# A two-layer decoder trunk: the order and the engines of norms, softmax weights and low parts

## The chip, the cores and the metric

The kernel runs on one core of a Trainium2 chip. A core has a matrix engine (TensorE, PE in the profile, with its weight loads as PEld), a vector engine (VectorE, DVE), an engine for activation functions (ScalarE, ACT), a general engine (GpSimd, POOL) and an engine that mostly issues transfers (SyncE, SP). They work side by side and wait for one another by semaphores. They share an on-chip memory (SBUF) of 128 partitions; matmuls write into eight accumulation banks (PSUM), each 128 partitions by 512 float32 values. The metric is the device time of one execution in microseconds (us), the median of several runs; lower is better.

## The reference, cut to what matters

```python
def ffn(h, w_in, w_out):            # four of these, each added with weight 0.5
    g, u = split(h @ w_in, 2)       # 1024 -> 2 x 2816
    return (silu(g) * u) @ w_out

for i in range(2):                  # 512 tokens, 1024 features, float32
    h = h + 0.5 * ffn(rmsnorm(h, nw[0]), ...)
    hn = rmsnorm(h, nw[1])
    h = h + (retention(hn) if i == 0 else forgetting_attention(hn))
    h = h + 0.5 * ffn(rmsnorm(h, nw[2]), ...)
    gate = sigmoid(rmsnorm(h, nw[3]) @ ple_w_gate[i])
    h = h + gate * (p[i] @ ple_w_proj[i])      # 256 -> 1024
return rmsnorm(h, final_norm_w)
```

Retention has four heads, with queries and keys of 256 and values of 512 features. Queries and keys are rotated by position, each head's output is normalised by its own root mean square over its 512 features (`rmsnorm(o, gn_w)`), multiplied by `silu(g)` and projected back. Forgetting attention has sixteen heads of 64 features: softmax over `q k^T * 64^-0.5 + c[query] - c[key]`, where `c` is a running sum of the logarithms of forget gates, causal, times `v`, and projected back.

## The kernel before, in words

Activations lie transposed, eight blocks of 128 features by 512 tokens (`h`, `hall`). Every matmul operand is split into a high part, rounded to the fast matmul type (float32r), and a low part that holds the rest; a product is three matmuls, high times high, high times low and low times high (`mm3`, L298 to L300). `split` (L289, L290) makes the parts of an activation: ScalarE copies the high part, VectorE subtracts. A third form with a scale is L292, L293.

The order of the whole is feed-forward 0, retention, feed-forward 1, gated input 0, feed-forward 2, forgetting attention, feed-forward 3, gated input 1 (in two halves of the tokens), final norm. TensorE executes in the order in which the program is written. The instructions of the other engines, whose queues are also worked off in order, are ordered by a planner that goes by its own estimate of when their inputs are ready.

**Weights** come through a class that holds the plan, a list of all weight chunks in the order of use (`W.plan`). A chunk of 128 x 1024 is loaded by a transfer that SyncE issues into one of four raw buffers (`wraw`), ScalarE casts its high part (L78), and VectorE or GpSimd, whichever `W.low` names at that point, subtracts for the low part (L79). There are three buffers of split chunks (`w8`), so the preparation runs two chunks ahead (`LOOKAHEAD`).

**Feed-forward input products** use a Strassen-Winograd form: `product` (L480) multiplies by a weight pair (`Pair`: the quarters q and r of a 1024 x 256 slab, with VectorE sums of them, `emit_sums`, L140, L78 and L79 on `sums`), in the steps `start`, `one`, `two`, `three`, `finish`. L530 to L533 and L546 to L548 are the sums on results, in place in the bank. Before them come a few pairs in the plain form (`plain`, L511; two in layers 0, 2 and 3, none in layer 1). There are 22 pairs of each layer, used up in chunks, and after each chunk the output products (`out_blocks`, L572, L575). A pair's low part is made in one of two ways: a *direct* pair by L79, like a chunk; any other by a ScalarE copy of the high part (L116), a ScalarE negation into the low half (L117) and an accumulating transfer that GpSimd issues, which adds the raw weights from HBM (L118). Direct are the first Winograd pair of a layer and one pair at each border of chunks.

**Norms** (`Norm`): squares are summed over the feature blocks by VectorE and GpSimd (`acc`, L414), split, and summed over the partitions by eight small matmuls with a vector of ones, 128 tokens each (`columns`, L428), so that the result has tokens on partitions, four columns (128 x 4). L459 and L452 to L456 form the inverse root there: two steps of Newton's kind behind ScalarE's root and VectorE's reciprocal (L453). `rows` then spreads the columns over partitions by four matmuls with a diagonal (`spread`, L447) into a bank, which ScalarE copies (L441) to a 128 x 512 tile `n.r`.

**Retention** goes head by head: q and k products and their rotation (`rotate`, L703 to L705), values (`v_part`, L683 to L685), the gates (`gate`, L781, L783), scores, chunk outputs `os` in four banks, the sum of their squares (`squares`, L715, L719), `head_scale`, then `outputs` (L810, L814 and a split). In `head_scale` two matmuls with a full matrix of ones over 512 columns (`over_features`, L310, L311) leave the sum in every partition, and the whole inverse root runs on 128 x 512 tiles; EPS, scaled by the token's mean square, is kept as a tile `epsv`. `early` is the number of gates ahead of `os`. Heads 2 and 3 are projected back together (`OutBoth`: `first` with head 2's half of the features, `rest` with head 3's and the additions to `h`, L669). `outputs` of a head come after the next head's first products.

**Attention** runs in eight passes `p` of two heads each. A pass multiplies out keys (`k_part`: L909 scales the result by `n.r` into a temporary tile in SBUF, L913 and L914 cast the high part, L915 subtracts) and queries (`q_part`: L925, L931, L932 likewise), then the scores (L948 with the low parts of the keys, L951), with four query blocks of 128, 256, 384 or 512 keys for each head. In `softmax` VectorE subtracts the row of `c` and takes the maximum on the way (L970, L974, custom instructions), flips the maximum's sign (L979), ScalarE takes the exponential with a running sum (L980), VectorE takes the reciprocal (L981) and scales the weights (L982). TensorE turns the weights (L997), L289 and L290 split them, and `attend` multiplies them by the values (L1010, L1011; L1013, L1014 combine the parts). Between these steps stand those of the next pass, with the preparation of its weights.

**The gated input** (`ple`): a gate block is a product of the normed `h` with `ple_gate` (24 matmuls), its own block a product of `p` with `ple_proj` (two feature blocks, six matmuls), and `rest` scales the gate by `n.r`, takes the sigmoid (L1089) and adds the product to `h` (L1093). In the first part gates 0 and 1 come ahead of `columns` and gate 2 ahead of `rows`, and each own product stands in its `rest`. `final_scale` and the final norm (L1129, L1146 to L1154) follow in layer 1.

## Time and profile before

| what | value |
|---|---|
| runs, us | 2286.51, 2284.73, 2275.85 |
| median of the runs, us | 2284.73 |
| profiled execution, its own time, us | 2285.92 |
| its span, first to last instruction, us | 2284.1 |
| mean granted clock of TensorE | 0.978 |
| busy, share of the span | PE 95%, DVE 67%, ACT 52%, POOL 20% |
| bytes read from HBM | 266.91 MB, 118 GB/s over the span |

The profile comes from one execution recorded by the hardware. A row of the timeline gives the start and the length in us, the engine, the line of the kernel, the operation, output and inputs with their shapes, how many instructions the row joins, and in square brackets how long the engine had been idle before and what it waited for. A row of the groups gives total busy time and the mean of one in ns, then the idle time before them. A row of the windows gives a stretch, its length, the busy us of PE, PEld, DVE, ACT and POOL with their instructions, the granted clock of TensorE (1.00 is full speed), the busy share of the transfer engines and GB/s. Matmuls overlap, so that the length of one is more than the distance between two.

### The profile page before, as it was taken

The page shows a single profiled execution, that of the slowest core. Times are in us where ns is not written, and L with a number is a line of the kernel's source. Part 1 is how long each engine was busy: PE and PEld are TensorE (multiplying, and loading weights), DVE is VectorE, ACT ScalarE, POOL GpSimd, SP SyncE. Part 2 cuts the span into 40 slices and gives each one's busy share as a digit, 9 for nine tenths or more (in the row PEclk, how much of TensorE's full clock was granted, in tenths as well). Part 3 has the DMA queues.
Part 4 walks back from the last instruction along what each step waited for, and adds up shares of the span by engine and source line. Part 5 has one row for each costly group of instructions (what it writes and reads, how often), then busy time and mean ns, then how long its engine had stood idle before and what let it go on. Part 6 is the DMA issues. An engine that isn't in the chain of part 4 may idle for free.

```text
span 2284.1 us, 34483 instructions
## 1 busy us (share of the span) xinstructions
PE 2170.2 (95%) x13465; PEld 1950.0 (85%) x13465; DVE 1530.0 (67%) x2775; ACT 1195.3 (52%) x1993; POOL 453.6 (20%) x339
## 2 busy tenths in 40 slices
PE   7999999999999899999998999999899989999998
PEld 7898997888888798989877898988777789989978
DVE  8676766374463976767675676765886776867674
ACT  7464553433333673646465464644665564645553
POOL 0010013444343010101100010113323100101044
PEclk8999999999999999999998999999899999999999
DMA  6465563222222474646333464653222144655531
GB/s 185 106 168 146 144 158 93 81 95 83 93 83 75 120 164 130 159 125 159 113 97 100 126 161 133 157 128 98 85 74 79 61 120 116 167 139 144 147 102 38
DMA packets 86610, 271.26 MB, mean 119 GB/s; under 512 B 9504, under 2 KB 13088, under 8 KB 86448
## 3 DMA queue, kind: packets, MB, share of 16 engines
q1 hardware_dynamic: 63328, 209.78, 28.0%
q0 software_dynamic: 21888, 58.21, 15.1%
q8 instruction: 105, 1.72, 0.3%
q10 hardware_dynamic: 1232, 1.09, 0.1%
q14 instruction: 57, 0.47, 0.1%
HBM read 266.91 MB, written 2.13 MB: 118 GB/s over the span
## 4 chain that ended last, share of the span: by engine, by line
PE 76%; DVE 11%; ACT 5%; DMA 4%; issue 3%; POOL 1%; SPq 0%; ACTq 0%; DVEq 0%; POOLq 0%
PE bank L480 29%; PE bank L300 13%; PE bank L298 13%; PE bank L299 13%; DMA wraw<-in_ffn_w_in 3%; PE bank L511 2%; PE bank L683 2%; PE bank L684 2%; PE bank L685 2%; DVE sums L140 1%; DVE w L79 1%; DMA w<-in_ffn_w_in 1%; ACT w L116 1%; ACT w L117 1%; ACT s L78 1%
## 5 line engine op out<-in xcount | busy, mean ns | idle before, releaser
L78 ACT CAST w<-wraw 128x1024 fp32r<-128x1024 f32 (+1 forms) x233 | 236.0, 1021 | 428.4 <-PE bank L300 275.0
L79 DVE TENSOR_TENSOR s<-sums,s 128x512 fp32r<-128x512 f32 x328 | 221.9, 686 | 133.6 <-ACT s L78 133.0
L78 ACT CAST s<-sums 128x512 fp32r<-128x512 f32 x328 | 199.0, 617 | 183.8 <-DVE sums L140 116.0
L300 PE MATMUL bank<-unit_a,w 128*128 128x512 f32 x736 | 287.0, 390 | 4.3 <-DVE w L79 2.6
L298 PE MATMUL bank<-unit_a,w 128*128 128x512 f32 x736 | 287.9, 391 | 1.6 <-ACT w L78 1.6
L299 PE MATMUL bank<-unit_a,w 128*128 128x512 f32 x736 | 286.6, 389 | 0.2 <-DVE unit_a L290 0.2
L298 PE MATMUL bank<-unit_d,w 128*128 128x512 f32 (+1 forms) x728 | 276.4, 380 | 3.5 <-ACT w L78 1.8
L299 PE MATMUL bank<-unit_d,w 128*128 128x512 f32 (+1 forms) x728 | 275.3, 378 | 4.0 <-DVE unit_d L293 2.9
L300 PE MATMUL bank<-unit_d,w 128*128 128x512 f32 (+1 forms) x728 | 274.6, 377 | 2.7 <-DVE w L79 2.7
L79 POOL TENSOR_TENSOR w<-wraw,w 128x1024 fp32r<-128x1024 f32 x89 | 218.7, 2460 | 282.9 <-ACT w L78 271.0
L118 POOL DMA_DIRECT2D a<-in_ffn_w_in x82 | 72.0, 878 | 680.0 <-ACT a L117 573.7
L480 PE MATMUL bank<-unit_b,s 128*128 128x256 f32 x904 | 193.1, 280 | 0.0
L480 PE MATMUL bank<-unit_a,s 128*128 128x256 f32 x1314 | 188.5, 281 | 1.9 <-ACT unit_a L358 1.0
L480 PE MATMUL bank<-unit_d,s 128*128 128x256 f32 x1140 | 181.8, 280 | 0.0
L79 DVE TENSOR_TENSOR w<-wraw,w 128x1024 fp32r<-128x1024 f32 (+1 forms) x144 | 168.5, 1176 | 18.7 <-ACT w L78 18.4
L572 DVE SCALAR_TENSOR_TENSOR tmp<-bank,rows 128x512 f32<-128x512 f32 x96 | 66.1, 690 | 164.4 <-PE bank L300 161.8
L118 POOL DMA_DIRECT2D w<-in_ffn_w_in x70 | 61.3, 875 | 578.1 <-ACT w L117 498.1
L480 PE MATMUL bank<-unit_b,w 128*128 128x256 f32 x738 | 139.5, 289 | 37.2 <-ACT tmp L532 22.8
L480 PEld LDWEIGHTS bank<-unit_a,s 128*128 128x128 f32 x1314 | 169.8, 192 | 2.7 <-ACT unit_a L358 1.2
L300 PEld LDWEIGHTS bank<-unit_a,w 128*128 128x128 f32 x736 | 138.1, 188 | 35.3 <-DVE w L79 4.3
L298 PEld LDWEIGHTS bank<-unit_d,w 128*128 128x128 f32 x728 | 139.7, 192 | 30.9 <-ACT w L78 3.4
L298 PEld LDWEIGHTS bank<-unit_a,w 128*128 128x128 f32 x736 | 138.3, 188 | 31.9 <-ACT w L78 3.5
(277 smaller groups left out, 4918.5 us busy)
## 6 DMA issues: line engine op xcount, KB each, us to landing
wraw<-in_ffn_w_in SPq DMA_DIRECT2D x174, 512.0 KB, 4.4
w<-in_ffn_w_in POOLq DMA_DIRECT2D x70, 512.0 KB, 5.6
wraw<-in_ffn_w_out SPq DMA_DIRECT2D x64, 512.0 KB, 4.7
a<-in_ffn_w_in POOLq DMA_DIRECT2D x82, 256.0 KB, 6.3
wraw<-in_ffn_w_out SPq DMA_DIRECT2D x32, 384.0 KB, 3.7
wraw<-in_ret_qk SPq DMA_DIRECT2D x16, 512.0 KB, 3.4
wraw<-in_ret_v SPq DMA_DIRECT2D x16, 512.0 KB, 3.6
wraw<-in_ret_g SPq DMA_DIRECT2D x16, 512.0 KB, 3.5
```

The lines of the kernel that those rows point to most:

```text
L78: self.nc.scalar.copy(hi, raw)
L79: self.low.tensor_tensor(out=lo, in0=raw, in1=hi.bitcast(F32), op=ALU.subtract)
L118: self.nc.gpsimd.dma_start(out=lo, in_=src, accum_op=ALU.add)
L298: nc.tensor.matmul(out, wh, xh, start=first, stop=False)
L299: nc.tensor.matmul(out, wh, xl, start=False, stop=False)
L300: nc.tensor.matmul(out, wl, xh, start=False, stop=last)
L480: add = lambda w, x, start, stop: nc.tensor.matmul(out, w, x, start=start, stop=stop, skip_group_check=True)
L511: nc.tensor.matmul(o[:, HALVES[t]], x[:, ks], y, start=k == t == q == 0, stop=k == KB - 1 and q == 2, skip_group_check=True,)
L572: nc.vector.scalar_tensor_tensor(out=t1, in0=o, scalar=-0.5, in1=n.r, op0=ALU.mult, op1=ALU.mult)
L683: nc.tensor.matmul(os[t], xh, wh[:, js], start=k == 0, stop=False)
L684: nc.tensor.matmul(os[t], xh, wl[:, js], start=False, stop=False)
L685: nc.tensor.matmul(os[t], xl, wh[:, js], start=False, stop=k == KB - 1)
```

## The change

1. In each feed-forward layer the pair after each direct pair becomes direct too, which makes twelve more: the second Winograd pair of each layer and eight at borders of chunks. VectorE's L79 takes the place of L117 and L118.
2. In part 0 of a gated input the own products of the first three blocks come before the gates, `columns` comes after gate 2, gate 3 comes ahead of `rows`, and the own product of block 3 after it. The plan of the weights follows.
3. In retention `head_scale` works on columns, as `Norm` does: eight small matmuls (`over_tokens`), an inverse root on 128 x 4, and after the head's last gate a spread and a ScalarE copy (`on_rows`). `epsv` becomes `epsc` on columns. `head_scale` stands before the last gate in heads 0 and 3, before gate 2 in heads 1 and 2; head 0 has one gate ahead of `os` rather than two. In head 3 the first products of `OutBoth` start before its last gates, two of four output chunks of them, and the plan of the weights follows.
4. In attention the scaled q and k stay in their banks (`t1 = o`), so that L909 and L925 work in place and the casts and subtractions read PSUM. The scale of q is negative; the masks add and take the minimum, and the exponential has scale −1, so the flip of sign (L979) goes. The scaling of the weights (L982) goes from VectorE to ScalarE.

```diff
-            ins[m].direct = True
+            ins[m].direct = ins[m + 1].direct = True
...
     def plan_ple(l):
-        for m in range(KB):
-            W.plan.append(ple_g[l][m])
-            if m in (2, 4):
-                W.plan.append(ple_p[l][m // 4])
+        W.plan += [ple_p[l][0]] + ple_g[l][0:5] + [ple_p[l][1]] + ple_g[l][5:8]
...
-    for h in range(RH):
+    for h in range(RH - 1):
         W.plan += ret_qk[h] + ret_v[h]
-        if 0 < h < RH - 1:
+        if h > 0:
             W.plan += ret_o[h - 1]
         W.plan += ret_g[h]
-    W.plan += ret_o[RH - 2][0:2] + ret_o[RH - 1][0:2]
+    W.plan += ret_qk[RH - 1] + ret_v[RH - 1] + ret_g[RH - 1][0:2] + ret_o[RH - 2][0:1] + ret_g[RH - 1][2:4]
+    W.plan += ret_o[RH - 2][1:2] + ret_o[RH - 1][0:2]
...
-    def over_features(hi, lo):
+    def over_tokens(parts):
         total = bank()
-        nc.tensor.matmul(total, ones_r, hi, start=True, stop=False)
-        nc.tensor.matmul(total, ones_r, lo, start=False, stop=True)
-        return total
+        for j in range(NT):
+            for i, part in enumerate(parts):
+                nc.tensor.matmul(
+                    total[:, 2 * j : 2 * j + 2], part[:, j * P : (j + 1) * P], ones_r[:, 0:2],
+                    start=i == 0, stop=i == 1,
+                )
+        return total[:, 0 : 2 * NT : 2]
...
             def head_scale(hi, lo):
-                total = over_features(hi, lo)
-                v, t = temp(), temp()
+                total = over_tokens((hi, lo))
+                v, t, rn = (pool.tile([P, NT], F32, name=x) for x in ("rv", "rt", "rn"))
                 nc.vector.scalar_tensor_tensor(
-                    out=v, in0=total, scalar=1.0 / S, in1=epsv, op0=ALU.mult, op1=ALU.add
+                    out=v, in0=total, scalar=1.0 / S, in1=epsc, op0=ALU.mult, op1=ALU.add
                 )
-                rn = pool.tile([P, S], F32, name="rn")
                 rsqrt(rn, v, t)
                 return rn
+            def on_rows(rn):
+                rows = pool.tile([P, S], F32, name="rnrows")
+                nc.scalar.copy(rows, spread(rn))
+                return rows
...
-                early = 0 if 0 < hd < RH - 1 else 2
+                early = (1, 0, 0, 2)[hd]
...
                 acc = squares(os)
-                for c in range(early, early + 2):
+                before, y = y, ([], [])
+                if hd == RH - 1:
+                    both = OutBoth([(ret_o[RH - 2], *before), (ret_o[RH - 1], *y)], nxt)
+                    both.first((0, 1))
+                for c in range(early, 4):
+                    if c == (3 if hd in (0, RH - 1) else 2):
+                        rn = head_scale(*acc)
                     gate(c)
-                rn = head_scale(*acc)
-                for c in range(early + 2, 4):
-                    gate(c)
-                before, y = y, ([], [])
+                rn = on_rows(rn)
...
-            both = OutBoth([(ret_o[RH - 2], *before), (ret_o[RH - 1], *y)], nxt)
-            both.first(range(4))
+            both.first((2, 3))
             outputs()
...
-                t1 = temp()
+                t1 = o
                 nc.vector.tensor_tensor(out=t1, in0=o, in1=n.r, op=ALU.mult)
...
-                t1 = temp()
+                t1 = o
                 nc.vector.scalar_tensor_tensor(
-                    out=t1, in0=o, scalar=H ** -0.5, in1=n.r, op0=ALU.mult, op1=ALU.mult
+                    out=t1, in0=o, scalar=-(H ** -0.5), in1=n.r, op0=ALU.mult, op1=ALU.mult
                 )
...
-                                op0=ALU.subtract, op1=ALU.max, accum_out=col(0),
+                                op0=ALU.add, op1=ALU.min, accum_out=col(0),
...
-                        nc.vector.tensor_scalar(out=col(2), in0=col(1), scalar1=-1.0, scalar2=None, op0=ALU.mult)
-                        nc.scalar.activation(t1, t1, AF.Exp, bias=col(2), accum_out=col(3))
-                        nc.vector.reciprocal(col(4), col(3))
-                        nc.vector.tensor_scalar(out=t1, in0=t1, scalar1=col(4), scalar2=None, op0=ALU.mult)
+                        nc.scalar.activation(t1, t1, AF.Exp, bias=col(1), scale=-1.0, accum_out=col(2))
+                        nc.vector.reciprocal(col(3), col(2))
+                        nc.scalar.activation(t1, t1, AF.Identity, scale=col(3))
...
-                def rest(m, g):
+                def added(m):
...
                     for k in range(2):
                         ks = slice(((m % 4) * 2 + k) * P, ((m % 4) * 2 + k + 1) * P)
                         mm3(o, wp[0][:, ks], wp[1][:, ks], phi[k][:, ts_], plo[k][:, ts_], k == 0, k == 1)
+                    return o
...
                 if part == 0:
+                    os = [added(m) for m in range(3)]
                     gs = gates((0, 1))
-                    n.columns()
                     W.low = nc.gpsimd if nxt.forms is None else nc.vector
                     gs += gates((2,))
+                    n.columns()
+                    gs += gates((3,))
                     n.rows()
-                    for m, g in enumerate(gs):
-                        rest(m, g)
-                    m = 3
+                    os.append(added(3))
+                    for m in range(4):
+                        rest(m, gs[m], os[m])
+                    m = 4
                 while m < KB:
-                    rest(m, gates((m,))[0])
+                    g = gates((m,))[0]
+                    rest(m, g, added(m))
```

More of the change, by code (lines that the diff above doesn't have):

```diff
@@ L423, in columns @@
         def columns(self):
-            total = bank()
-            for j in range(NT):
-                for i, part in enumerate(self.acc_parts):
-                    nc.tensor.matmul(
-                        total[:, 2 * j : 2 * j + 2], part[:, j * P : (j + 1) * P], ones_r[:, 0:2],
-                        start=i == 0, stop=i == 1,
-                    )
+            total = over_tokens(self.acc_parts)
             self.c = stat.tile([P, NT], F32, name="cols")
@@ L434, in columns @@
             t = stat.tile([P, NT], F32, name="ct")
-            mean_eps(self.v, total[:, 0 : 2 * NT : 2])
+            mean_eps(self.v, total)
             rsqrt(self.c, self.v, t)
@@ L696, in retention @@
             rk2 = pool.tile([P, NT], F32, name="rk2")
-            epsv = pool.tile([P, S], F32, name="epsv")
+            epsc = pool.tile([P, NT], F32, name="epsc")
             def rotate(x1, x2):
@@ L740, in retention @@
                     n.columns()
+                    nc.vector.tensor_scalar(out=epsc, in0=n.v, scalar1=EPS, scalar2=None, op0=ALU.mult)
                     nc.vector.tensor_tensor(out=rk2, in0=n.c, in1=n.c, op=ALU.mult)
@@ L750, in retention @@
                     n.rows()
-                    nc.scalar.mul(epsv, spread(n.v), EPS)
                 v = []
@@ L961, in scores @@
                     )
-                    st = pool.tile([P, 5 * NT], F32, name=f"sm{e}")
+                    st = pool.tile([P, 4 * NT], F32, name=f"sm{e}")
                     mine = [None] * NT
@@ L1086, in rest @@
                         mm3(o, wp[0][:, ks], wp[1][:, ks], phi[k][:, ts_], plo[k][:, ts_], k == 0, k == 1)
+                    return o
+                def rest(m, g, o):
                     t1, t2, hm = temp()[:, :w], temp()[:, :w], h[m][:, ts_]
```

6 lines of the change are left out of this document (3 added, 3 removed).

## The prediction, made before the changed kernel ran

> **What bounds the kernel now.** I read the page's summary first, then TensorE's own waits, then the stretches in which the waits lie.
>
> ```profile
> span 2284.1 us, 34483 instructions
> ...
> PE 2170.2 (95%) x13465; PEld 1950.0 (85%) x13465; DVE 1530.0 (67%) x2775; ACT 1195.3 (52%) x1993; POOL 453.6 (20%) x339
> ...
> PE 76%; DVE 11%; ACT 5%; DMA 4%; issue 3%; POOL 1%; SPq 0%; ACTq 0%; DVEq 0%; POOLq 0%
> ```
>
> TensorE (PE) is busy 95% of the span and carries 76% of the chain that ended last. It is idle for 2284 − 2170 = 114 us; only there, and where its clock is halved, can time be won. The list of what TensorE waited for (total us, times, longest) begins with:
>
> ```profile
> PE bank L480 <- ACT tmp L532: 29.6, 18, 2.8
> PE bank L480 <- DMA w<-in_ffn_w_in: 14.4, 4, 4.6
> ```
>
> The largest entry, 29.6 us in 18 waits, belongs to the Winograd sums of the feed-forward layers, which the change leaves alone. The second is one of the four that the change touches: these DMA waits, the waits of the attention's scores, and the two gated inputs. The profiled execution took 2285.9 us, 1.8 more than its span and 1.2 above the median of the runs, 2284.7; I sum against 2285.9 and don't correct for the 1.2. About 0.5% (11.4 us) is what can be told from no change.
>
> **Part 1, more direct low parts.** In a weight pair that isn't direct, ScalarE negates into the low half (L117) and a DMA that GpSimd issues adds the raw weights (L118). TensorE waits for that DMA; here are three of the four waits from its timeline, and what the engines did in the stretches behind them (columns: length, then busy us of PE, PE's weight loads, DVE, ACT, POOL, then the granted clock):
>
> ```profile
> 43.80 0.62 PE L480 MATMUL bank<-unit_b,w 128*128 128x256 f32 x3 [2.81 <-DMA w<-in_ffn_w_in]
> 1238.33 0.80 PE L480 MATMUL bank<-unit_b,w 128*128 128x256 f32 x2 [4.56 <-DMA w<-in_ffn_w_in]
> 1876.92 0.50 PE L480 MATMUL bank<-unit_b,w 128*128 128x256 f32 x2 [4.18 <-DMA w<-in_ffn_w_in]
> ```
> ```profile
> 1235.90:1242.70 6.80, 4.37 (x20) 4.37 (x21) 1.28 (x3) 0.64 (x2) 0.00 (x0) 0.50 0.62 161
> 1877.60:1881.00 3.40, 3.40 (x18) 3.40 (x17) 0.10 (x1) 0.75 (x2) 0.00 (x0) 0.50 0.49 169
> 2212.10:2222.30 10.20, 7.59 (x35) 7.50 (x36) 5.07 (x6) 4.00 (x5) 7.51 (x4) 0.50 0.01 2
> 44.60:58.30 13.70, 9.47 (x44) 8.81 (x43) 8.46 (x19) 5.94 (x10) 0.00 (x0) 0.50 0.41 136
> ```
> ```profile
> L79 DVE TENSOR_TENSOR w<-wraw,w 128x1024 fp32r<-128x1024 f32 (+1 forms) x144 | 168.5, 1176 | 18.7 <-ACT w L78 18.4
> ```
>
> These waits (2.81, 4.56, 4.18 us) are for the second direct pair of layers 0, 2 and 3. Each gives way to one VectorE subtraction (L79) of 1.18 us, and ScalarE's L117 goes. The granted clock is 0.50 around and behind the waits, so half of the busy 4.37 and 3.40 us is lost as well.
> Layer 2: VectorE is busy 1.28 of 6.80 us, so the subtraction fits. The most it gives is 4.56 + 2.2 = 6.7; I take 5.6, the subtraction being on the path now, with 0 as the other end (a later weight late by as much). Layer 3: 4.18 + 1.7 = 5.9 at most, I take 5.0. Layer 0: behind the wait VectorE is busy 8.46 of 13.70 us and TensorE idle for 4.2 more, so at the kernel's start other steps come just as late. I take −0.5, between +1.2 (the subtraction on the path) and −7.5 (2.81 and half of the slow 9.47).
> The other pairs, in mid-layer, show no wait but the fourth of that list, which stays. Eight of 1.18 us go to VectorE, whose idle share (67% busy) hides them; without that cover they cost up to 4, and with eight DMAs less on GpSimd's queue they might gain as much. I take 0.
>
> **Part 2, attention.** One pass of eight, then VectorE's groups and ScalarE's over the whole stage, then the end of another pass:
>
> ```profile
> 1742.30:1765.00 22.70, 20.52 (x101) 17.21 (x101) 21.45 (x75) 14.70 (x33) 6.40 (x4) 0.92 0.22 70
> ```
> ```profile
> L982 DVE TENSOR_SCALAR p<-p,sm 128x256 f32<-128x256 f32 (+1 forms) x64 | 37.3, 585 | 0.5
> ...
> L932 DVE TENSOR_TENSOR q<-tmp,q 64x512 fp32r<-64x512 f32 x14 | 20.6, 1474 | 5.3 <-ACT q L931 5.1
> ...
> L1014 DVE TENSOR_TENSOR tmp<-bank,tmp 64x512 f32<-64x512 f32 x14 | 9.6, 683 | 0.4
> L979 DVE TENSOR_SCALAR sm<-sm 128x1 f32<-128x1 f32 x64 | 9.0, 140 | 0.0
> ```
> ```profile
> L980 ACT ACTIVATE p<-p,sm 128x256 f32<-128x256 f32 (+1 forms) x64 | 35.5, 556 | 32.5 <-DVE sm L979 32.5
> L78 ACT CAST w<-wraw 128x1024 fp32r<-128x1024 f32 x22 | 23.1, 1051 | 30.1 <-issue 13.9 <-PE bank L685 9.3 <-POOL unit_c L957 5.3
> ```
> ```profile
> 1779.31 2.37 POOL L79 TENSOR_TENSOR w<-wraw,w 128x1024 fp32r<-128x1024 f32 x1 [2.81 <-ACT w L78]
> 1779.95 3.00 DVE L932 TENSOR_TENSOR q<-tmp,q 64x512 fp32r<-64x512 f32 x2 [0.74 <-ACT q L931]
> 1782.98 1.40 DVE L1014 TENSOR_TENSOR tmp<-bank,tmp 64x512 f32<-64x512 f32 x2
> ```
> ```profile
> L948 PE MATMUL bank<-klo,q 128*128 128x256 f32 (+1 forms) x64 | 26.6, 432 | 17.8 <-DVE tmp L1014 9.0 <-DVE tlo L290 3.2 <-DVE unit_b L293 3.0
> L530 DVE TENSOR_TENSOR bank<-bank,tmp 128x256 f32<-128x256 f32 x82 | 34.9, 426 | 3.6 <-PE bank L480 3.6
> ```
>
> VectorE is busy 21.45 of 22.70 us: it is this stage's pace. Its low part of q (L932) reads two SBUF tiles and takes 1.47 us in the mean; at 1779.95 a pair of them runs beside GpSimd's subtraction and takes 3.00. L1014, of the same size with one operand in a PSUM bank, keeps to 0.68. With the scaled q in PSUM, L932 has L1014's operands, so I price it at 0.69: 14 × (1.47 − 0.69) = 11 us less. Scaling in place in a bank has its row in L530, 0.43 us for 256 columns at 128 partitions, no more than from SBUF, so the write costs nothing. New is that the banks of q and k are held until the low parts are read, some 2 us longer; no row shows what that costs, and between nothing and a wait of 2 us in each of seven passes I take nothing, no wait for a bank being in the list now.
>
> The weights' scaling (L982, 37.3 us) and the sign change (L979, 9.0) leave VectorE, 57 us with the 11, or 7 a pass. ScalarE gets 64 scalings, which I price as its exponentials on the same tiles, 0.556: 35.6, or 4.4 a pass, and 14.70 become 19.1. That is below the pass's 22.70, but ScalarE works in order, and each scaling waits for VectorE's reciprocal; queued behind it are the casts of the turned weights (L289), for which TensorE waits, and the next weights (L78).
>
> TensorE's idle before the scores' matmuls (L948) is 17.8 us, of which 3.0 for v's parts stay. About two thirds of the other 14.8 can go (10; the scores still need q's casts), and at a granted clock of 0.92 a further 0.08 × 20.5 = 1.6 a pass is lost, or 11 over seven passes, most of it behind these gaps: 18 to 20 in full. Against it I book 1.1 us in each of seven passes for ScalarE's late casts, since its idle of 8.0 has to take up 4.4 in order: −11. The ends are −20 and +2 × 7 = +14 (the banks).
>
> **Part 3, retention.** The chain of waits, TensorE's timeline and VectorE's load at layer 1's start:
>
> ```profile
> 736.04 3.37 DVE rn L453
> 400.19 0.79 PE bank L428 x8
> 422.90 0.87 PE bank L447 x8
> ```
> ```profile
> 745.47 0.50 PE L298 MATMUL bank<-unit_d,w 128*128 128x512 f32 x1 [1.70 <-ACT unit_d L289]
> 782.00:800.00 18.00, 13.64 (x96) 13.15 (x95) 16.33 (x36) 12.20 (x24) 1.75 (x2) 0.88 0.68 178
> ```
>
> In each head two matmuls over 512 columns become eight small ones (0.79 us, as L428's) and a spread of four (half of 0.87). The two cost 0.44 at the pace shown below, so +0.8 a head, less the one spread of EPS that goes (0.43): +2.7 for TensorE. VectorE's chain on 512 columns, whose reciprocal alone takes 3.37, becomes one on four columns, so the last head's outputs come sooner and TensorE's wait of 1.70 for them goes. Layer 1's newly direct pair falls where VectorE is busy 16.33 of 18 us: +1.2. Together 2.7 − 1.7 + 1.2 = +2; ends −3 (the slower clock there, 0.88, goes too) and +4 (the new order of the last head's weights makes one late by an L79 or two).
>
> **Part 4, the gated inputs.**
>
> ```profile
> 1150.00:1170.00 20.00, 20.00 (x92) 16.57 (x91) 14.39 (x23) 12.10 (x18) 0.00 (x0) 1.00 0.25 85
> 1170.00:1190.00 20.00, 19.84 (x90) 16.32 (x89) 18.17 (x34) 14.35 (x26) 0.00 (x0) 1.00 0.26 91
> 1197.45 0.38 PE L511 MATMUL bank<-unit_d,w 128*128 128x256 f32 x1 [3.15 <-ACT unit_d L366]
> 2211.07 0.38 PE L299 MATMUL bank<-unit_d,w 128*128 128x256 f32 x1 [2.92 <-DVE unit_d L293]
> ```
> ```profile
> 2212.86 0.37 PE L428 MATMUL bank<-ones_r,tmp 128*128 128x2 f32 x1 [0.94 <-ACT tmp L289]
> 2215.09 1.65 PE L428 MATMUL bank<-ones_r,tmp 128*128 128x2 f32 x7 [1.85 <-DVE tmp L290]
> ```
>
> Layer 0's: TensorE runs full at 20.00 / 92 = 0.22 us a matmul. Three own products (18 matmuls, 4.0) come first, and gate 3 (24, 5.2) moves ahead of the spread: the row scales come 9.2 us later. In the first window VectorE does 14.39 of 20, so 6.6 in 9.2, less one L79: 5.4 us that have to go behind, where it is busy 18.17 of 20 and where TensorE already waits 3.15 at the next layer's start. So +5.4 if all lands on the end, 0 if VectorE's idle takes it up, +8 if the halved clock follows; I take 4.
>
> Layer 1's works on half the tokens at a time. TensorE waits 2.92, 0.94 and 1.85 = 5.7 around the squares' sums, and loses half of the busy 7.59 us in the slow stretch after them (third of the windows above), 3.8. The new order has half of 4.0 of own products and half of 5.2 of a gate to put there, 4.6. What is late next is the spread, with nearly all banks held by four products and four gates. I take −6, ends 0 and −9.5.
>
> **Sum.** −0.5 − 5.6 − 5.0 + 0 − 11 + 2 + 4 − 6 = −22.1 against 2285.9: 2264 us.
>
> **Rivals.**
> - Attention gives nothing: what VectorE saves goes to later ScalarE casts and held banks, and L948 waits as long for another engine. For it: VectorE's waits before L932 (5.1 us) are for ScalarE's cast. Against it: GpSimd's subtraction is what stretches L932, and PSUM operands don't suffer from it. It gives 2264 + 11 = 2275, within 0.5% of the median. The Trainium skill, "VectorE: DVE Perf Modes", section "Rules for kernel authors", is on its side: accept the slow rate on a PSUM source, or copy to SBUF first if many operations follow, and the change undoes just such a copy. This trace differs for these operations: 0.68 from PSUM, 1.47 in the mean from SBUF.
> - ScalarE becomes the bound of the attention. It has 19.1 us a pass; if its idle for the exponentials' input (32.5 us, 4.1 a pass) and before the weights' casts (30.1, 3.8) stays in full, a pass takes 27.0 against 22.7: +4.3 × 7 = +30, and in place of −11 that gives 2305, slower. It decides when more than 3.6 of those 7.9 us stay. Against it: the 4.1 are waits for VectorE's sign change, which goes.
> - Attention in full: 2264 − 9 = 2255 or less.
> - The waits go but the halved clock stays, because smaller waits in the same places keep it: what I booked for it, 1 in layer 2, 1 in layer 3, 1.5 in layer 1's gate and 4 in attention, falls away: 2271.5.
>
> **How the numbers follow.** The forecast (2250 to 2274) gets 0.55, attention without gain 0.18, attention in full 0.10, ScalarE bound 0.10, the clock kept 0.07. Faster: 0.55 + 0.10 + 0.07, less 0.04 for the forecast's upper edge, 0.68; same 0.18 + 0.04 = 0.22; slower 0.10. Low end: attention in full (−9), layer 0's good end (−7) and layer 1's gate in full (−3.5), 2264 − 19.5 = 2244. High end: attention without gain (+11), mid-layer +4, layer 0's gate +4, retention +2: 2285. Beyond it lies ScalarE as the bound.
>
> **What would show it.** Right: one DMA wait of L480 is left of four, L932 is at 0.69 throughout, L948's idle is under half, L982 stands on ScalarE at 0.55, no wait for squares in layer 1's gate, longer waits at layer 2's start. Wrong: L948 waits for ScalarE's casts, ScalarE is idle 6 us or more of a longer pass, TensorE waits for a weight in the last head, or VectorE's added subtractions open waits at L480 in mid-layer.

## The result: faster by 1.5%, by a way that the prediction had put at nothing

| | before | after |
|---|---|---|
| median, us | 2285.6 (four runs) | 2251.1 (four runs, 2250.2 to 2254.6) |
| ratio, 95% interval | | 0.9854 [0.9814, 0.9894] |
| span of the profiled execution, us | 2284.1 | 2252.8 |

2264 was forecast, 2244 to 2285 as the range. The time lies in it, but most of the gain comes from a place with a forecast of zero. The page of the changed kernel, the lines that answer to those of before:

```profile
span 2252.8 us, 34423 instructions
...
PE 2158.8 (96%) x13501; PEld 1940.0 (86%) x13501; DVE 1467.5 (65%) x2661; ACT 1211.5 (54%) x2050; POOL 436.7 (19%) x326
...
PE 78%; DVE 8%; ACT 6%; issue 3%; DMA 3%; POOL 1%; SPq 0%; DVEq 0%; ACTq 0%; POOLq 0%
```

TensorE is idle for 94 us, not 114, and busy 11 us less, though it executes 36 matmuls more: less of its time runs at the halved clock (the mean granted clock is 0.983 in this profile, 0.978 before). What it waited for (line numbers are of the changed kernel: L476 was L480, L528 was L532):

```profile
PE bank L476 <- ACT tmp L528: 11.1, 7, 3.2
PE bank L443 <- DVE cols L452: 10.0, 2, 6.8
PE bank L298 <- DVE w L79: 9.5, 10, 3.7
PE bank L507 <- ACT unit_d L368: 4.9, 1, 4.9
...
PE bank L476 <- DMA w<-in_ffn_w_in: 2.8, 1, 2.8
```

The DMA waits went from four to one, as forecast. The next entries are waits for VectorE's column scales, for low parts of weights and for normed activations, mostly where a stage starts; the longest of them are taken up below. But the list's first entry of before, 29.6 us in 18 waits for a copy that the change doesn't touch, went to 11.1 in seven. To see where the time went I cut both timelines at TensorE's first and last matmul of each stretch. "Booked" is what the prediction had put there; the rest of the span, mostly the output products between the chunks, took as long in both within 0.2 us.

| stretch, us | before | after | difference | booked |
|---|---|---|---|---|
| layer 0 to the end of its first chunk of products | 94.4 | 94.3 | −0.1 | −0.5 |
| layer 0, second and third chunk | 82.5, 76.7 | 77.6, 74.8 | −6.7 | 0 (mid-layer) |
| retention's first values to layer 1's spread | 404.6 | 410.6 | +6.0 | +2 (with the next) |
| layer 1, first chunk | 68.0 | 70.7 | +2.7 | |
| layer 1, second and third chunk | 82.7, 54.3 | 85.5, 54.1 | +2.5 | 0 (mid-layer) |
| end of layer 1's products, gated input 0, to layer 2's spread | 130.4 | 138.1 | +7.7 | +4 |
| layer 2, first chunk | 49.0 | 42.4 | −6.6 | −5.6 |
| layer 2, second and third chunk | 82.7, 78.0 | 77.6, 73.4 | −9.6 | 0 (mid-layer) |
| attention, first values to layer 3 | 261.1 | 250.7 | −10.4 | −11 |
| layer 3, first chunk | 48.1 | 44.1 | −4.0 | −5.0 |
| layer 3, second and third chunk | 84.0, 78.1 | 77.6, 73.4 | −11.1 | 0 (mid-layer) |
| end of layer 3's products, gated input 1, to the end | 117.6 | 116.0 | −1.6 | −6 |

### The profile page after: what moved, and what is told of

It is laid out like the page before. It is cut to its first block, busy times and chain, and to the rows that moved or that the text cites. A ratio compares the mean times of both kernels' runs of the same rounds, so it can differ in the third digit from the quotient of the medians.

```text
span 2252.8 us, 34423 instructions
## 1 busy us (share of the span) xinstructions
PE 2158.8 (96%) x13501; PEld 1940.0 (86%) x13501; DVE 1467.5 (65%) x2661; ACT 1211.5 (54%) x2050; POOL 436.7 (19%) x326
## 4 chain that ended last, share of the span: by engine, by line
PE 78%; DVE 8%; ACT 6%; issue 3%; DMA 3%; POOL 1%; SPq 0%; DVEq 0%; ACTq 0%; POOLq 0%
PE bank L476 30%; PE bank L298 13%; PE bank L296 13%; PE bank L297 13%; DMA wraw<-in_ffn_w_in 3%; PE bank L507 2%; PE bank L679 2%; PE bank L680 2%; PE bank L681 2%; DVE w L79 1%; DVE sums L140 1%; ACT p L982 1%; ACT w L78 1%; POOL w L79 1%; ACT p L984 1%
## 5 line engine op out<-in xcount | busy, mean ns | idle before, releaser
L78 ACT CAST w<-wraw 128x1024 fp32r<-128x1024 f32 (+1 forms) x245 | 248.6, 1022 | 456.0 <-PE bank L298 276.0
L79 DVE TENSOR_TENSOR s<-sums,s 128x512 fp32r<-128x512 f32 x328 | 220.4, 685 | 90.6 <-ACT s L78 90.1
L298 PE MATMUL bank<-unit_d,w 128*128 128x512 f32 (+1 forms) x712 | 270.2, 380 | 6.4 <-DVE w L79 6.4
L296 PE MATMUL bank<-unit_d,w 128*128 128x512 f32 (+1 forms) x712 | 271.2, 381 | 2.8 <-ACT w L78 1.8
L79 POOL TENSOR_TENSOR w<-wraw,w 128x1024 fp32r<-128x1024 f32 x90 | 217.0, 2414 | 287.2 <-ACT w L78 275.3
L297 PE MATMUL bank<-unit_d,w 128*128 128x512 f32 (+1 forms) x712 | 270.2, 379 | 1.8 <-DVE unit_d L288 1.8
L79 DVE TENSOR_TENSOR w<-wraw,w 128x1024 fp32r<-128x1024 f32 (+1 forms) x155 | 179.5, 1164 | 40.2 <-ACT w L78 40.0
L118 POOL DMA_DIRECT2D a<-in_ffn_w_in x82 | 71.8, 876 | 684.9 <-ACT a L117 531.8
L476 PE MATMUL bank<-unit_b,s 128*128 128x256 f32 x904 | 191.3, 278 | 0.0
L476 PE MATMUL bank<-unit_a,s 128*128 128x256 f32 x1314 | 188.4, 281 | 2.0 <-ACT unit_a L360 1.0
L476 PE MATMUL bank<-unit_d,s 128*128 128x256 f32 x1140 | 179.0, 277 | 0.0
L476 PEld LDWEIGHTS bank<-unit_a,s 128*128 128x128 f32 x1314 | 169.8, 192 | 3.0 <-ACT unit_a L360 1.2
L298 PEld LDWEIGHTS bank<-unit_a,w 128*128 128x128 f32 x736 | 138.2, 188 | 36.1 <-DVE w L79 5.3
L296 PEld LDWEIGHTS bank<-unit_a,w 128*128 128x128 f32 x736 | 138.3, 188 | 32.8 <-ACT w L78 4.5
L298 PEld LDWEIGHTS bank<-unit_d,w 128*128 128x128 f32 x712 | 136.0, 191 | 32.6 <-DVE w L79 8.3
L297 PEld LDWEIGHTS bank<-unit_a,w 128*128 128x128 f32 x736 | 138.3, 188 | 28.3 <-DVE unit_a L288 0.5
L296 PEld LDWEIGHTS bank<-unit_d,w 128*128 128x128 f32 x712 | 136.3, 191 | 30.2 <-ACT w L78 3.4
```

Source lines behind the costliest of these rows:

```text
L78: self.nc.scalar.copy(hi, raw)
L79: self.low.tensor_tensor(out=lo, in0=raw, in1=hi.bitcast(F32), op=ALU.subtract)
L118: self.nc.gpsimd.dma_start(out=lo, in_=src, accum_op=ALU.add)
L296: nc.tensor.matmul(out, wh, xh, start=first, stop=False)
L297: nc.tensor.matmul(out, wh, xl, start=False, stop=False)
L298: nc.tensor.matmul(out, wl, xh, start=False, stop=last)
```

## The experiments

The kernel before took 2283.5, 2284.8 and 2275.6 us (medians) in the three groups of comparisons, so kernels of different groups are compared by their ratio to it, and single stages by their stretch in the timeline.

### Mid-layer: which order ScalarE works in

In the second chunk of layer 0, ScalarE's timeline before shows the copy (L532) behind a cast of the next pair's weights (L116), its negation (L117) and a cast of a sum; TensorE's row shows the wait:

```profile
179.86 1.05 ACT L116 CAST w<-wraw 128x1024 fp32r<-128x1024 f32 x1
180.81 1.05 ACT L117 ACTIVATE w<-wraw 128x1024 fp32r<-128x1024 f32 x1
181.77 0.60 ACT L78 CAST s<-sums 128x512 fp32r<-128x512 f32 x1
182.28 0.36 ACT L532 COPY tmp<-bank 128x256 f32<-128x256 f32 x1
```
```profile
182.69 1.58 PE L480 MATMUL bank<-unit_a,w 128*128 128x256 f32 x11 [1.54 <-ACT tmp L532]
```

The cast is late because its raw weights are; the chain of waits leads there, one pair later:

```profile
184.50 5.41 DMA wraw<-in_ffn_w_in
...
191.37 1.04 ACT w L116
```

So there is a loop: load, sums, cast, copy behind the cast, TensorE's next products, release of the raw buffer, next load. In the changed kernel the same chunk has the copy first:

```profile
173.42 0.37 ACT L528 COPY tmp<-bank 128x256 f32<-128x256 f32 x1 [0.31 <-DVE bank L526]
174.01 0.62 ACT L287 CAST unit_d<-tmp 128x512 fp32r<-128x512 f32 x1 [0.22 <-DVE tmp L554]
174.53 1.05 ACT L116 CAST w<-wraw 128x1024 fp32r<-128x1024 f32 x1
```

Theory 1: this order, which the planner settles when the kernel is built, is the gain. Theory 2: the direct pair takes an accumulating transfer out. Two kernels tell them apart. The first is the kernel before with the preparation of the next weights moved, and no direct pair more:

```diff
...
-                    start(begun)
+                    start(begun, W.claim)      # takes the pair, prepares nothing
                     one(begun)
                     two(begun)
+                    W.refill()                 # now the next chunk and its sums
...
```

> The kernel before, with one thing moved: the next weight pair is prepared after a pair's products and first sums (steps one and two) are written, not ahead of them, in every chunk of all four feed-forward layers. No pair is made direct. ScalarE's queue then has the second copy of step two (L532 of before) ahead of the next pair's high cast (L116) nearly everywhere, where before it mostly stands behind it. Theory 1 (order in ScalarE's queue: the copy that TensorE needs stands behind a cast that waits for a transfer): the chunks of layers 0, 2 and 3 go at 9.6 us a pair instead of 10 to 13, the 29.6 us of waits for L532 fall under 10, and the time falls by 20 to 28 us to 2257 to 2265. Theory 2 (the transfers: what the direct pairs bring is one accumulating transfer less at the start of each chunk): order alone brings nothing, 2285 within 5.

Measured: 2251.2 us, ratio 0.9847 [0.9813, 0.9881], as much as the whole change and below the 2257 to 2265 expected: its second and third chunks together are 32.6 us shorter than before. Its ScalarE has the copy (L542) ahead of the cast, and the waits for it shrink; the DMA waits stay:

```profile
177.51 0.37 ACT L542 COPY tmp<-bank 128x256 f32<-128x256 f32 x1
177.78 1.06 ACT L116 CAST w<-wraw 128x1024 fp32r<-128x1024 f32 x1
```
```profile
PE bank L490 <- DMA w<-in_ffn_w_in: 14.8, 5, 4.7
...
PE bank L490 <- ACT tmp L542: 5.0, 3, 2.5
```

Layer 2's second chunk in the windows (length, busy PE, PEld, DVE, ACT, POOL), for the kernel before, the changed one and this one:

```profile
1314.20:1396.80 82.60, 78.31 (x674) 77.71 (x673) 62.79 (x112) 55.17 (x96) 12.25 (x14) 1.00 0.72 173
```
```profile
1319.60:1397.20 77.60, 77.60 (x674) 77.59 (x673) 63.21 (x115) 54.40 (x94) 11.35 (x13) 1.00 0.72 178
```
```profile
1302.00:1380.10 78.10, 77.95 (x674) 77.73 (x673) 65.21 (x115) 56.96 (x98) 12.22 (x14) 1.00 0.77 186
```

TensorE is idle for 4.3, 0.0 and 0.2 us. The moved kernel still has the 14 GpSimd instructions there of before, one more than the changed kernel, and its transfers are as many as before, at more GB/s (last column). Theory 2 falls as the account of this gain.

The second takes only the eight mid-layer pairs out of the changed kernel:

```diff
-            ins[m].direct = ins[m + 1].direct = True
+            ins[m].direct = True
+        ins[PLAIN[i] + 1].direct = True
```

> The changed kernel with only the first of its new direct pairs in each layer kept; the eight in mid-layer have their negated copy and accumulating transfer back. By the prediction's term (0, between -4 and +4) the time stays at 2251 within 4. By the two traces, in which the chunks behind the first of each layer are 24 us shorter after the change, all of that is given back: 2273 to 2277, with ScalarE's order and the waits for the copy as before.

Measured: 2270.4, ratio 0.9938 [0.9911, 0.9965]: 19 us are given back, less than the 22 to 26 expected, and ScalarE's order is that of before.

```profile
PE bank L477 <- ACT tmp L529: 22.8, 17, 2.5
```

The third adds the moved preparation to the changed kernel:

> The changed kernel with the next weight pair prepared after a pair's steps one and two in all four layers, as in the run that moved only this. If the order of ScalarE's queue is the cause of the waits for the second copy, the 11.1 us of them that are left go, layer 1's second chunk takes 77.6 us of 85.5 and its first 68 of 70.8: 2236 to 2241. If the direct pairs' gain and the order's are two different things that add up, still less: 2225 to 2232.

Measured: 2239.4, ratio 0.9812 [0.9795, 0.9829]. All second chunks take 77.6 and layer 1's first takes 68.0. So it isn't two gains that add up: where the changed kernel had the good order already, nothing is added.

The two kinds of chunk behave differently, and only the second chunks follow the direct pairs (us, layers 0, 2 and 3; the fourth kernel is the one of the section on retention):

| kernel | second chunks | third chunks |
|---|---|---|
| before | 82.5, 82.7, 84.0 | 76.7, 78.0, 78.1 |
| changed | 77.6, 77.6, 77.6 | 74.8, 73.4, 73.4 |
| changed, without the mid-layer pairs | 83.0, 84.4, 81.4 | 73.6, 75.3, 73.4 |
| changed, retention as before | 77.6, 77.6, 77.6 | 78.6, 78.0, 78.9 |
| before, preparation moved | 78.5, 78.1, 77.8 | 73.4, 73.4, 73.4 |

In a second chunk the cast stands between a pair's two copies four times before, twice in the changed kernel (without a wait there), and four times again without the mid-layer pairs. The 16.3 us that these chunks gain are there with the pairs and gone without them (16.0). In a third chunk the cast stands there three times in each of the first four kernels. The 11.1 us that the third chunks gain can't be put down to the direct pairs: they stay when the pairs are taken out, and in the fourth kernel they are gone although the pairs are in.

Two things stay open. Moving the preparation also reorders VectorE's and GpSimd's queues; that ScalarE's is the one that counts is read from the wait and the rows ahead of it, not shown apart. And it isn't settled why the third chunks differ at the same order on ScalarE. In layer 2's, a load behind the cast landed after 5.0 us in the changed kernel (issued at 1473.28, landed at 1478.33) and after 6.8 in the fourth (1474.59, 1481.36). Each is one profiled execution, so it can't be said whether the kernel or the execution makes the difference. With the copy first, the third chunks took 73.4 to 73.7 in all four kernels that have it.

### Attention: which of the two halves

The changed kernel's rows bear out the prices: the low part of q (now L934) at 0.689 for 0.69, the scalings on ScalarE (L984) at 0.551 for 0.556.

```profile
L934 DVE TENSOR_TENSOR q<-bank,q 64x512 fp32r<-64x512 f32 x14 | 9.6, 689 | 4.9 <-ACT q L933 4.7
L917 DVE TENSOR_TENSOR klo<-bank,khi 64x512 fp32r<-64x512 f32 x14 | 9.6, 688 | 15.5 <-ACT khi L916 15.5
```
```profile
L984 ACT ACTIVATE p<-p,sm 128x256 f32<-128x256 f32 (+1 forms) x64 | 32.8, 551 | 3.6 <-DVE sm L983 3.5
```

But the sum doesn't say which half did it. One kernel has q and k in PSUM and scales on VectorE with the sign flip:

```diff
...
-                        nc.scalar.activation(t1, t1, AF.Identity, scale=col(3))
+                        nc.vector.tensor_scalar(out=t1, in0=t1, scalar1=col(4), scalar2=None, op0=ALU.mult)
```

> The changed kernel with only half of the attention's change: q and k stay in PSUM, but the weights are scaled by VectorE and the sign flip is there, as before. From the first values to the end of the projection the stage took 261.1 us before and 250.7 after. Theory A (GpSimd's subtraction stretching VectorE's reads of two SBUF tiles is what made the gaps): this half gives most of it, the stage takes 252 to 254 and the kernel 2253. Theory B (VectorE's load as a whole makes them): this half removes 11 to 13 us of VectorE's 164, the other 46; the stage takes 257 to 259 and the kernel 2258.

The other keeps the scaling on ScalarE and copies q and k to SBUF:

```diff
...
-                t1 = o
+                t1 = temp()
...
```

> The changed kernel with the other half: the weights are scaled by ScalarE, but q and k are copied to SBUF with the positive scale, and the sign flip is there. Theory A: the low part of q still takes up to 2.3 us beside GpSimd; the stage takes 256 to 259 of its 250.7, the kernel 2257. Theory B: VectorE is relieved of 37 of 46 us, the stage takes 252 to 254 and the kernel 2253.

Measured: PSUM alone 2252.3, 0.9868 [0.9848, 0.9888], the whole effect; ScalarE's scaling alone 2277.4, 0.9969 [0.9956, 0.9983], 26 us worse than both together. The stage from its first scores to layer 3, in windows of before, after, PSUM alone and scaling alone:

```profile
1603.00:1842.10 239.10, 219.62 (x1042) 181.67 (x1041) 190.17 (x596) 147.93 (x317) 62.24 (x38) 0.94 0.24 76
```
```profile
1598.80:1827.50 228.70, 214.33 (x1041) 177.32 (x1040) 146.31 (x466) 173.71 (x382) 62.20 (x38) 0.97 0.25 79
```
```profile
1601.70:1826.20 224.50, 211.56 (x1041) 174.14 (x1041) 177.66 (x594) 145.94 (x318) 62.48 (x38) 0.98 0.25 81
```
```profile
1603.10:1852.00 248.90, 220.14 (x1041) 184.40 (x1041) 174.75 (x532) 175.25 (x381) 60.73 (x38) 0.93 0.23 73
```

With the scaling alone VectorE is relieved, 190 us to 175, and the stage is 9.8 longer than before. The rows of q's low part (shortest, median and longest in ns; first the kernel before, then the scaling alone with its group) and one pass's timeline show where the relief went: VectorE now reaches q's low parts when GpSimd's subtraction of weights runs. Of the two in each pass one was lengthened before, in seven of eight passes; now both are, in six. That the relief brought the two into step is read from these rows, not tested apart.

```profile
L932 DVE TENSOR_TENSOR q<-tmp,q x16: 685/687/2303, 1599.9 to 1782.3; 64x512 fp32r<-64x512 f32 x16
L934 DVE TENSOR_TENSOR q<-tmp,q 64x512 fp32r<-64x512 f32 x14 | 34.5, 2466 | 7.8 <-ACT q L933 7.5
L934 DVE TENSOR_TENSOR q<-tmp,q x16: 685/2456/2815, 1600.0 to 1790.7; 64x512 fp32r<-64x512 f32 x16
```
```profile
1646.63 2.37 POOL L79 TENSOR_TENSOR w<-wraw,w 128x1024 fp32r<-128x1024 f32 x1 [5.74 <-ACT w L78]
1649.47 2.34 POOL L79 TENSOR_TENSOR w<-wraw,w 128x1024 fp32r<-128x1024 f32 x1 [0.47 <-ACT w L78]
1647.10 5.26 DVE L934 TENSOR_TENSOR q<-tmp,q 64x512 fp32r<-64x512 f32 x2 [0.97 <-ACT q L933]
```

1.47 us in the mean before, 2.47 here, 0.69 from PSUM, though 14 of the changed kernel's 16 ran beside a GpSimd subtraction for most of their time. Theory A holds, and more strongly than it was put: from its first values the stage took 246.5 us with PSUM alone, where 252 to 254 were expected, and 270.9 with the scaling alone, where it was 256 to 259. The Trainium skill, "SBUF — State Buffer", section "Who interferes with whom", has the rule: a VectorE instruction with two SBUF inputs contends with a GpSimd instruction that reads SBUF, one with at most one SBUF input outside the two-port modes doesn't. These rows agree with both halves of it. Whether the scaling's move helps or harms once q is in PSUM can't be told: the stage took 246.5 and 248.7 us in two profiles without it, and 247.3 to 251.2 in nine with it.

### Retention and layer 1's start

> The changed kernel with retention as before (head scales on 128x512 rows, old order of the last head). Retention took 4.0 us more after the change and layer 1's start 4.7 more. Theory R1 (the columns' chain and the new order of the last head cost both): both go, 2251 - 8.7 = 2242. Theory R2 (layer 1's start is late because of its newly direct pair on VectorE): only retention's 4.0 goes, 2247, and the waits of 4.5 and 3.2 us at layer 1's start stay. By the prediction's own term (+2) it would be 2249.

Measured: 2258.3, 0.988 [0.9843, 0.9917]. The median lies above the changed kernel's, though the intervals overlap, and above all three numbers. The stage itself did get shorter: first values to layer 1's spread 407.4, against 410.6 with the change and 404.6 before. So retention's change costs 3.1, and 2.9 belongs to something else. What makes this profiled execution longer are the third chunks of the table above, +3.7, +4.6 and +5.4 us.

For the other 2.9, the changed kernel without the one new direct pair of layer 1:

```diff
-            ins[m].direct = ins[m + 1].direct = True
+            ins[m].direct = True
+            ins[m + 1].direct = i != 1 or m > 0
```

> The changed kernel without one of the twelve new direct pairs, the second pair of layer 1. From retention's first values to the end of layer 1's first chunk of products it takes 481.3 us after the change, 472.6 before, and 480.2 in the changed kernel with retention as before. Theory D (this pair's subtraction, which falls where VectorE is the late engine, costs most of the 8.7): it goes to 474 to 476 and the kernel to 2244 to 2246. Theory R (retention's new order does): it stays at 480 to 482, 2251. The prediction booked 1.2 for this pair.

Measured: 2250.6, 0.9898 [0.9871, 0.9924]: not told apart from the change. The stretch to the spread is 407.6, 3.0 less, so the pair costs that; but layer 1's first chunk stays long, 73.0, so that both together take 480.6 of the 481.3, the number that theory R had given, for another reason. That chunk took 68.0 before and in the kernels with the moved preparation. It goes with ScalarE's order: the cast stands between a pair's two copies twice there before, four times in the changed kernel, five times here and at most once with the preparation moved. The expected 2244 was a misreading of mine that put this part on the pair.

Then retention with columns, but the last head's order and plan as before:

```diff
-                if hd == RH - 1:
-                    both = OutBoth(...)
-                    both.first((0, 1))
...
-            both.first((2, 3))
+            both = OutBoth(...)
+            both.first(range(4))
```

> The changed kernel with the head scales on columns, but the last head's order and weight plan as before: four blocks of head 2's projection after the last gate, as cover for the scales and the outputs, not two before the gates and two after. If the cover is why TensorE's waits for the last head's outputs stayed (2.8 us both times): the waits shrink to under 1 and the kernel takes 2249. If the columns' chain is late anyway: 2251, waits as they are.

Measured: 2253.0, 0.989 [0.9859, 0.9921], the same as the change within the interval; in the stretch 406.6, 4.0 less. (The 2249 expected didn't come: in this profiled execution the third chunks took 77.9, 74.4 and 78.0.) TensorE's waits for the last head's outputs, five of them in the changed kernel (2.3 us in all; the first and the last are shown), become one:

```profile
741.87 0.50 PE L297 MATMUL bank<-unit_d,w 128*128 128x512 f32 x1 [0.65 <-DVE unit_d L288]
...
747.01 0.50 PE L297 MATMUL bank<-unit_d,w 128*128 128x512 f32 x1 [0.58 <-DVE unit_d L288]
```
```profile
745.50 0.50 PE L296 MATMUL bank<-unit_d,w 128*128 128x512 f32 x1 [0.78 <-DVE unit_d L287]
```

So the columns cost nothing (406.6 against 407.4), and the new order of the last head costs the 4.0. These waits account for 1.5 of it; that two blocks of cover behind the scales are too few fits them, and where the rest goes isn't shown.

### The gated inputs

At layer 2's start TensorE waited 3.2 and 2.5 us for normed activations before; now it waits three times, 11.7 us in all:

```profile
1204.95 0.38 PE L507 MATMUL bank<-unit_d,w 128*128 128x256 f32 x1 [3.48 <-ACT unit_d L360]
...
1212.10 0.58 PE L507 MATMUL bank<-unit_d,w 128*128 128x256 f32 x1 [4.89 <-ACT unit_d L368]
...
1217.87 2.16 PE L507 MATMUL bank<-unit_c,w 128*128 128x256 f32 x6 [3.32 <-ACT unit_c L360]
```

> The changed kernel with the gated inputs in the order of before, in both layers. By the traces layer 0's cost 7.7 us with the start of layer 2, and layer 1's gained 1.6: 2251 - 7.7 + 1.6 = 2245. By the prediction's terms (+4 and -6) 2253. If layer 2's waits at its start (3.5, 4.9, 3.3 us) come from the newly direct pair instead, they stay and the time is about 2252.

Measured: 2243.4, 0.9814 [0.9779, 0.9849], as expected from the traces. The stretch takes 131.1 instead of 138.1; the end takes 117.0 instead of 116.0.

The own products first, but the scales where they were:

```diff
                     gs = gates((0, 1))
+                    n.columns()
                     W.low = nc.gpsimd if nxt.forms is None else nc.vector
                     gs += gates((2,))
-                    n.columns()
-                    gs += gates((3,))
                     n.rows()
...
```

> The changed kernel with the gated inputs' first three own products still first, but the row scales where they were before (columns after gates 0 and 1, spread after gate 2; gate 3 and its own product behind). Layer 0's scales then come 4.0 us later than before in TensorE's order, not 9.2. If it is the lateness of the scales that costs 7.7 us there: 7.7 x 4.0 / 9.2 = 3.3 stays, 2251 - 4.4 = 2247, and layer 1's part is less good by a microsecond or so. If it is something else in the new order: 2251.

Measured: 2248.1, 0.9885 [0.986, 0.9909]; the stretch takes 135.8, so 2.3 of the 7.7 come back where 4.4 were expected. The lateness of the scales is part of the cost, not all of it; own products ahead of the gates cost as well, in a way that no run here shows.

### A version that beats both

The kernel before with the moved preparation, the attention's change and the second direct pair of layers 2 and 3:

> The kernel before with the moved preparation of weights, the attention's change, the second direct pair of layers 2 and 3 only, and nothing of the rest (retention and both gated inputs as before). From the run with the moved preparation, 2251: -10.4 for attention and -6.6 and -4.0 for the first chunks of layers 2 and 3 by the two traces: 2230, between 2226 and 2236, and so faster than the changed kernel.

Measured: 2229.9, 0.9767 [0.9744, 0.979], faster than the changed kernel.

```profile
PE bank L492 <- ACT tmp L544: 6.0, 3, 2.5
PE bank L312 <- DVE w L79: 5.3, 8, 0.7
```

> The best combination so far, 2230, with two more things: the attention's weights are scaled by VectorE again (q and k in PSUM alone took 246.5 us for the stage against 250.7 with both), and the gated input of layer 1 alone has the new order (1.6 us shorter after the change). 2230 - 3 or 4 - 1.6 = 2225, between 2219 and 2230. If the stage differences of single profiles are noise, 2230.

Measured: 2227.8, 0.9793 [0.9769, 0.9817]. The two combinations can't be told apart.

## Why the prediction was right, and where it was not

- **The sum.** The range held because errors cancelled, which is luck: mid-layer −24.9 where 0 was booked, against retention with layer 1's start +6.7, layer 0's gated input +3.7 and layer 1's +4.4 above what was booked. With the mid-layer term at its 0 the other measured terms give 2286 − 6 = 2280.
- **The step that failed** is "the Winograd sums of the feed-forward layers, which the change leaves alone". Their 29.6 us of waits were in a quoted row, the largest of the list. I asked what the change does to the waiting instruction's own work and not what stands ahead of it on ScalarE. The pairs "show no wait" because the wait stands at another line, the copy that queued behind them. The bounds of ±4 came from VectorE's idle share and GpSimd's queue and were about the wrong engines. The experiments put the second chunks' −16.3 in the queue's order, which the direct pairs change; the third chunks' −11.1 comes at the same order as before, and its cause stays open. Layer 1's second and third chunk took 2.5 more.
- **First chunks.** Layers 0, 2 and 3: −0.1, −6.6 and −4.0 for −0.5, −5.6 and −5.0; the DMA waits went as stated. Layer 2's −6.6 is more than its wait of 4.56, so the rival that keeps the halved clock doesn't hold there; layer 3's −4.0 is less than its 4.18. In layer 0 the wait behind it, for the column scales, is the longest now, 6.8 us (the second row of the list of waits; 3.6 before), which is why nothing came of it there, as forecast.
- **Attention.** −10.4 for −11, with both prices right. The mechanism was right for q in PSUM, which alone gives all of it. The split was wrong: of the 57 us taken from VectorE the 46 of scaling and sign flip gave nothing, and the scaling without PSUM was a loss in this stage. The terms behind the −11 were too large, and that they still met is luck: TensorE's idle before the scores' matmuls fell by 4.9 (17.8 to the 12.9 of the row below) where 10 was taken, not to under half, and its busy time in the stage by 5.3 where up to 11 was taken for the clock; what of the 7.7 set against them for ScalarE's late casts came can't be told. The rival "attention gives nothing" falls. The rule that it had on its side, in the Trainium skill, "VectorE: DVE Perf Modes", section "Rules for kernel authors", leaves a choice between reading PSUM at the slow rate and copying to SBUF first for many operations. Here the copy lost: 0.689 from PSUM, and from SBUF 0.685 only where no neighbour runs.

```profile
L950 PE MATMUL bank<-klo,q 128*128 128x256 f32 (+1 forms) x64 | 24.4, 396 | 12.9 <-DVE unit_b L291 4.1 <-DVE tlo L288 3.6 <-DVE klo L917 1.9
```

- **ScalarE as the bound.** It didn't come: its work went from 148 to 174 us over the stage, and its idle took it up.
- **Retention.** Mis-sized: +2 for +6.0, and +2.7 behind it. The −1.7 didn't come: in the new order the waits for the last head's outputs are 2.3 us, not none. The order costs 4.0 where nothing was booked, and the pair at layer 1's start 3.0 for 1.2; the columns, booked at +2.7 and −1.7, came to −0.9.
- **Layer 0's gated input.** +7.7, at the end (+8) of what was given, not at the 4 taken.
- **Layer 1's gated input.** Mis-sized: −1.6 for −6. The three waits went, but the wait moved ahead, to the own products' weights: VectorE's subtraction for them, which TensorE's longest wait for L79 (3.7 us) ends with, is queued behind an addition that takes 2.19 us beside GpSimd.

```profile
2175.49 2.55 POOL L79 TENSOR_TENSOR w<-wraw,w 128x1024 fp32r<-128x1024 f32 x1 [0.27 <-ACT w L78]
```
```profile
2176.40 2.19 DVE L571 TENSOR_TENSOR hall<-hall,tmp 128x512 f32<-128x512 f32 x1
2178.51 1.21 DVE L79 TENSOR_TENSOR w<-wraw,w 128x1024 fp32r<-128x1024 f32 x1
```

## What to carry to other kernels

When a wait names a short copy, read what stands ahead of that copy on its engine; a cast that waits for a transfer makes every later instruction of an in-order queue wait with it, and a change that seems to be about bytes may act by moving it. Emit the work that feeds the bottleneck before the work that prepares the next round, and look at the queue's order in the trace rather than at the program. Price the halves of a change separately, since one may hide that the other loses.

## What the runs showed of the hardware that I had not expected

VectorE's subtraction of two SBUF tiles took 2.47 us in the mean, up to 2.82, beside GpSimd's subtraction, against 0.69 with one operand in PSUM beside the same neighbour. In the pass shown, VectorE's two subtractions ended 0.55 us behind GpSimd's second one. With VectorE relieved of the weights' scaling, the mean went from 1.47 to 2.47 us. The same raw load of 512 KB took 5.0 us in one kernel's profiled execution and 6.8 in another's, at the same place of the same order; with the cast ahead of the copy, the chunk took 4.6 us longer in the second.
